# Delta-rule rounds: the small TensorE groups laid in 16 slots, TensorE held to the program order, two PSUM tiles for the group products

## The chip, the cores and the metric

The kernel runs on one core of one Trainium2 chip. The metric is the device time of that core in microseconds (us), the median of the runs. TensorE does the matmuls, VectorE and ScalarE the elementwise work, GpSimd a little setting to zero, and SyncE (SP) issues the DMAs.

## The reference

Two transformer blocks follow each other over 512 positions of width 1024. The change lies in the first block's gated delta rule (8 heads, 8 chunks of 64 positions):

```python
h = rms_norm(x, norm1_w) * (1 + scale1) + shift1
proj = h @ w_in
qkv = silu(causal_dwconv(concatenate([dn_q, dn_k, dn_v]), dn_conv_w))
...
a_mat = where(strict, einsum('bhncd,bhnjd->bhncj', k_beta, kc) * decay, 0.0)
sol = triangular_solve(eye + a_mat, rhs, left_side=True, lower=True, unit_diagonal=True)
u, w = sol[..., :dv], sol[..., dv:]
...
def step(state, inp):                      # over the 8 chunks
    qe_i, att_i, u_i, w_i, kd_i, dec_i = inp
    v_new = u_i - w_i @ state
    o_i = qe_i @ state + att_i @ v_new
    state = state * dec_i + kd_i.T @ v_new
    return state, o_i
...
o_a = rms_norm(o_a, dn_norm_w) * silu(dn_z)
y_a = o_a @ w_out_dn
```

Beside it stand the modulation vector of the block (`silu(c) @ w_ada + b_ada`), an attention, the feed-forward part, and the second block; these are as they were.

## The kernel before

**Dense work.** A projection (`proj`) makes a 128x512 tile in PSUM from 8 steps over the width, each of three matmuls, since weights and activations are split into a high and a low part (`mm3`, lines 307 to 310: `hi` with `hi`, `hi` with `lo`, `lo` with `hi`). I call each of these 24 a dense matmul. `wload` loads a weight tile (512 KB) on SP's queue into one of two `raw` buffers, ScalarE makes `hi` and VectorE `lo` (L295).

**Delta-rule stage.** It runs in six rounds, t = 0 to 5. Heads go in pairs p = 0 to 3. Round t holds the projections of pair t (six tiles in rounds 0 to 3, four gate tiles in 4 and 5, two more `z` tiles from round 2 on), the preparation of pair t-1 (`pre_steps`, rounds 1 to 4), and the recurrence over the chunks of pair t-2 (`chain_steps`, rounds 2 to 5). Parts of the modulation vector are interleaved (`ada_steps`, L338: `adraw` tiles on VectorE).

**Preparation of a pair.** `estep` and `sums` make decays and norms; `kkstep(b)` (b = 0, 1 for the two halves of four chunks) makes the products `kk` of keys and queries on half the array (L608), and VectorE the matrix `C` from them. The triangular solve starts from 16x16 blocks: `kkstep` writes these blocks of `C` to DRAM in 8 small DMAs per half, `load_bk` loads them as `BK`, turned so that one partition holds one block; `subst` inverts them in 15 steps of two VectorE instructions (L659 and L661, in place in `UK`); `wback` copies the transpose `XK` and writes `UK` and `XK` to DRAM, and loads both back into block-diagonal tiles by 32 small DMAs on SP's queue (`U` and `Xb` alternately, 16 for b = 0, then 16 for b = 1). `lvl_steps(b)` then builds the 64x64 inverse from the blocks: `s0` multiplies `Cl16` (a copy of parts of `C`) with `Xb`, `s1`, `s2`, `s3` and `s2` again follow, and `s5` and `s6` give `ut` and `wt`; each is a group `pp` of four 128-wide matmuls (L689). `tk` and `tv` transpose keys and values (`tpk`, `tpv`).

**Recurrence of a pair.** `state(c)` makes `pw` = `wt` times state and `pc` = query times state (L762, L769, half the array each); VectorE makes `vn`. `update(c)` makes `ss` (L779) and the second part of `pc` (L789); VectorE and ScalarE make the next state `S` and the output `o`. `post` normalises `o` and transposes it (`tpo`).

**What sets the order.** `merge` (line 196) gives every step of several lists a place between 0 and 1 and calls them in the order of these places; a projection tile is one step, 24 dense matmuls in a row. In its call (line 840) `pr`, the preparation up to `wback`, is spread over 0 to 0.68 of the round, `l0` = `lvl_steps(0)` over 0.7 to 1, and `late`, the `lvl_steps(1)` of the round before, over 0.04 to 0.27. Behind that, the scheduler of the framework orders the instructions on each engine anew, as it finds them ready. PSUM has one bank each for `ppre` (all of `kk`, `tpk`, `tpv`, `pp`), `pst`, the two tags of `pch` (`pw` and `pc`), and two each for `psS` and the dense tiles.

## Time and profile before

| what | value |
| --- | --- |
| median of 3 runs | 2168.42 us (2167.34 to 2168.75) |
| the profiled execution | 2166.97 us, span 2165.2 us |
| TensorE (PE) busy | 2135.2 us, 99% of the span |
| weight loads (PEld) | 1722.0 us, 80% |
| VectorE (DVE) | 1202.5 us, 56% |
| ScalarE (ACT) | 898.0 us, 41% |
| mean granted clock of TensorE | 0.995 |

Matmuls are pipelined, so that a record overlaps the next; what a matmul costs is read from start to start. Weight loads run beside the matmuls. Of the time from start to end TensorE is idle for 30 us, and most of that lies at the two ends. The delta-rule stage takes 380.5 us of the span.

### The profile page before, as it was taken

The numbers are of one execution on the slowest core, as the hardware profiler recorded it, in microseconds if no ns is written. First come the engines' busy times: TensorE is split into PE (matmuls) and PEld (weight loads), VectorE is DVE, ScalarE is ACT, GpSimd is POOL, SyncE is SP. The second block draws the span as 40 slices with busy tenths as digits, with TensorE's granted clock in tenths as the row PEclk, the third lists the DMA queues.
The fourth block names the chain that finished last, engine by engine and source line by source line (L and its number), as shares of the span: only waits on it lengthen the run. The fifth ranks groups of instructions, "written<-read, shape, count | busy, mean of one in ns | idle before, by whom it ended". The sixth has DMA issues, their size and how long they took to land.

```text
span 2165.2 us, 27498 instructions
## 1 busy us (share of the span) xinstructions
PE 2135.2 (99%) x10636; PEld 1722.0 (80%) x10636; DVE 1202.5 (56%) x2243; ACT 898.0 (41%) x1479; POOL 17.8 (1%) x49
## 2 busy tenths in 40 slices
PE   7999999999999999999999999999999999999997
PEld 3787877778888878888888887887778888888886
DVE  4777667465554554444335898545544454334446
ACT  5645443465553353333224323634443343224333
POOL 1000000000000000000000000000000000000000
PEclk9999999999999999999999999999999999999999
DMA  8533334222224343333333222232222433333332
GB/s 312 167 109 115 90 91 131 61 67 69 73 71 129 105 136 94 96 95 95 95 100 117 80 83 83 74 98 83 84 78 82 148 97 98 96 98 97 92 96 77
DMA packets 89579, 219.86 MB, mean 102 GB/s; under 512 B 23384, under 2 KB 28648, under 8 KB 88808
## 3 DMA queue, kind: packets, MB, share of 16 engines
q1 hardware_dynamic: 89448, 218.10, 33.0%
q8 instruction: 84, 1.38, 0.3%
q14 instruction: 47, 0.39, 0.1%
HBM read 211.50 MB, written 7.08 MB: 101 GB/s over the span
## 4 chain that ended last, share of the span: by engine, by line
PE 90%; DVE 5%; ACT 2%; issue 1%; DMA 1%; SPq 0%; DVEq 0%; ACTq 0%
PE mm L308 25%; PE mm L310 25%; PE mm L309 24%; PE pp L689 2%; DVE yc L1265 1%; DVE lo L295 1%; PE bpo L1593 1%; PE po L1041 1%; PE tps L1202 1%; PE tps L1203 1%; PE tps L1204 1%; PE ssp L571 1%; PE pw L762 1%; PE pc L789 1%; PE ss L779 1%
## 5 line engine op out<-in xcount | busy, mean ns | idle before, releaser
L294 ACT ACTIVATE hi<-raw 128x1024 fp32r<-128x1024 f32 (+3 forms) x354 | 351.5, 994 | 779.0 <-PE mm L309 690.4
L295 DVE TENSOR_TENSOR lo<-raw,hi 128x1024 fp32r<-128x1024 f32 (+3 forms) x354 | 403.8, 1141 | 439.0 <-ACT hi L294 427.9
L308 PE MATMUL mm<-H,hi 128*128 128x512 f32 x856 | 341.8, 400 | 4.7 <-ACT hi L294 1.7
L310 PE MATMUL mm<-H,lo 128*128 128x512 f32 (+1 forms) x856 | 340.5, 398 | 0.5 <-DVE lo L295 0.5
L309 PE MATMUL mm<-H,hi 128*128 128x512 f32 (+1 forms) x856 | 340.0, 397 | 0.0
L308 PEld LDWEIGHTS mm<-H,hi 128*128 128x128 f32 x856 | 161.4, 189 | 41.2 <-issue 3.0
L310 PEld LDWEIGHTS mm<-H,lo 128*128 128x128 f32 (+1 forms) x856 | 161.4, 189 | 36.1 <-issue 3.4
L309 PEld LDWEIGHTS mm<-H,hi 128*128 128x128 f32 (+1 forms) x856 | 161.5, 189 | 33.9 <-issue 2.7
L308 PE MATMUL mm<-XN,hi 128*128 128x512 f32 (+1 forms) x456 | 180.0, 395 | 0.0
L309 PE MATMUL mm<-XN,hi 128*128 128x512 f32 (+1 forms) x456 | 179.6, 394 | 0.0
L310 PE MATMUL mm<-XN,lo 128*128 128x512 f32 (+1 forms) x456 | 179.3, 393 | 0.0
L310 PEld LDWEIGHTS mm<-XN,lo 128*128 128x128 f32 (+1 forms) x456 | 85.1, 187 | 19.3 <-issue 1.7
L308 PEld LDWEIGHTS mm<-XN,hi 128*128 128x128 f32 (+1 forms) x456 | 85.1, 187 | 18.8 <-ACT hi L294 0.9
L309 PE MATMUL mm<-HN,hi 128*128 128x512 f32 x256 | 100.0, 391 | 0.0
L308 PE MATMUL mm<-HN,hi 128*128 128x512 f32 x256 | 99.6, 389 | 0.0
L310 PE MATMUL mm<-HN,lo 128*128 128x512 f32 x256 | 99.6, 389 | 0.0
L308 PE MATMUL mm<-F,hi 128*128 128x512 f32 x256 | 99.6, 389 | 0.0
L309 PE MATMUL mm<-F,hi 128*128 128x512 f32 x256 | 99.6, 389 | 0.0
L310 PE MATMUL mm<-F,lo 128*128 128x512 f32 x256 | 99.6, 389 | 0.0
L309 PEld LDWEIGHTS mm<-XN,hi 128*128 128x128 f32 (+1 forms) x456 | 84.9, 186 | 17.8 <-issue 1.3
L1265 DVE SCALAR_TENSOR_TENSOR yc<-cp,cdh,yc 128x512 f32<-128x512 f32 x120 | 89.9, 750 | 2.9
L308 PE MATMUL mm<-FF,hi 128*128 128x512 f32 x176 | 68.5, 389 | 0.0
(662 smaller groups left out, 3817.1 us busy)
## 6 DMA issues: line engine op xcount, KB each, us to landing
raw<-in_w_ff SPq DMA_DIRECT2D x64, 512.0 KB, 3.6
raw<-in_ffn_up SPq DMA_DIRECT2D x44, 512.0 KB, 3.6
raw<-in_w_dn SPq DMA_DIRECT2D x32, 512.0 KB, 3.8
adraw<-in_w_adaT SPq DMA_DIRECT2D x64, 256.0 KB, 3.2
raw<-in_w_ga SPq DMA_DIRECT2D x32, 512.0 KB, 3.7
raw<-in_w_br SPq DMA_DIRECT2D x32, 256.0 KB, 2.7
raw<-in_ffn_down SPq DMA_DIRECT2D x16, 448.0 KB, 3.4
X<-in_xT SPq DMA_DIRECT2D x4, 1024.0 KB, 7.2
```

The source lines that it names most:

```text
L294: nc.scalar.activation(out=hi, in_=src, func=AF.Copy)
L295: nc.vector.tensor_tensor(out=lo, in0=src, in1=hi.bitcast(F32), op=ALU.subtract)
L308: nc.tensor.matmul(ps, wh, xh, start=start, stop=False)
L309: nc.tensor.matmul(ps, wh, xl, start=False, stop=False)
L310: nc.tensor.matmul(ps, wl, xh, start=False, stop=stop)
L571: nc.tensor.matmul(ssp[64 * h:64 * h + 64, kind * 8 + c:kind * 8 + c + 1], sq[:, c], C("ones", 0, 1), start=True, stop=True)
L689: nc.tensor.matmul(pp[:, c4], lh[:, c4], rh[:, c4], start=True, stop=True)
L762: nc.tensor.matmul(pw[64 * h:64 * h + 64], st["wt"][b][:, c4, 64 * h:64 * h + 64], S[:, h], start=True, stop=True)
L779: nc.tensor.matmul(ss, st["kd"][b][64 * h:64 * h + 64, c4], vn[64 * h:64 * h + 64], start=True, stop=True)
L789: nc.tensor.matmul(pc[:, 0], ATT[(2 * p + b) % 4][:, c4], vn, start=True, stop=True)
L1041: nc.tensor.matmul(po[:, qs], VT[:, kb, hh], pT[:, kb * P:kb * P + P], start=(kb == 0), stop=(kb == qb))
L1265: i = nc.vector.scalar_tensor_tensor(out=ycs[m], in0=cps[m][:, s:s + T], scalar=cdh[:, m * 31 + s:m * 31 + s + 1], in1=ycs[m], op0=ALU.mul ...
```

## The change

Seven things are edited, all in the delta-rule stage.

1. `k_steps` cuts each projection tile into 8 steps of three dense matmuls.
2. `in_slots` takes the place of `merge` in rounds 1 to 5: a round has 16 slots. At the start of a slot come the small steps that a list names for it, in the order turns, chain, late levels, preparation, first levels, modulation; then a sixteenth of the dense steps (9 dense matmuls per slot in rounds 1, 4 and 5, 12 in rounds 2 and 3).
3. The places: `kkstep` in slots 2 and 3, `load_bk` 3, `subst` 4 to 7, `wback` 8, `lvl_steps(0)` from slot 10 to 14, `lvl_steps(1)` in slots 0 to 4 of the next round, and one step of the recurrence per slot.
4. `pin(True)` wraps TensorE's matmul and transpose, from round 1 to 5, so that the scheduler keeps them in the order of the program. The other engines are still ordered by the scheduler.
5. `ppre` has two buffers.
6. `pw` becomes a part of the `pc` tile, in one bank, and the `pc` product is issued ahead of it.
7. `post` is split: the transposes `tpo` become `turn`, which runs in slot 0 of the next round and takes its PSUM tile from `ppre`.

```diff
@@ -449,7 +449,7 @@
     dB = dctx.enter_context(pool("dB"))
...
     pst = dpx.enter_context(pool("pst", 1, PS))
-    ppre = dpx.enter_context(pool("ppre", 1, PS))
+    ppre = dpx.enter_context(pool("ppre", 2, PS))
     pch = dpx.enter_context(pool("pch", 1, PS))
@@ -521,8 +521,20 @@
     ST = [dict() for _ in range(4)]
...
-    def conv_silu(widx, dst):
-        ps = proj(PRE.pop(widx, A["w_dn"][widx]), H)
+    def k_steps(src, done):
+        st = {}
+        def one(k):
+            if k == 0:
+                st["w"] = src if isinstance(src, tuple) else wload(src, KD, P)
+                st["ps"] = PSM[0].tile([P, T], F32, tag="mm", name="mm")
+            mm3(st["ps"], st["w"][0][:, k], st["w"][1][:, k], H[0][:, k], H[1][:, k], k == 0, k == KD - 1)
+            if k == KD - 1:
+                done(st["ps"])
+        return [lambda k=k: one(k) for k in range(KD)]
+    def conv_silu(widx, dst, ps):
         acc = dA.tile([P, T], F32, tag="cacc", name="cacc", bufs=2)
@@ -533,30 +545,34 @@
     def proj_steps(p):
...
-        def one(kind, h):
+        def one(kind, h, ps):
             if "KQ" not in st:
...
             if kind == 0:
-                conv_silu(8 + 2 * p + h, st["KQ"][:, :, h])
+                conv_silu(8 + 2 * p + h, st["KQ"][:, :, h], ps)
             elif kind == 1:
-                conv_silu(2 * p + h, st["KQ"][:, :, 2 + h])
+                conv_silu(2 * p + h, st["KQ"][:, :, 2 + h], ps)
             else:
-                conv_silu(16 + 2 * p + h, st["vf"][:, :, h])
-        return [lambda kind=kind, h=h: one(kind, h) for kind in range(3) for h in range(2)]
+                conv_silu(16 + 2 * p + h, st["vf"][:, :, h], ps)
+        def tile_steps(kind, h):
+            w = (8, 0, 16)[kind] + 2 * p + h
+            done = lambda ps: one(kind, h, ps)
+            return k_steps(PRE.pop(w, A["w_dn"][w]), done)
+        return [tile_steps(kind, h) for kind in range(3) for h in range(2)]
...
-        def one(h):
+        def one(h, zps):
             zs = dB.tile([P, T], F32, tag=f"zs{h}", name=f"zs{h}")
-            zps = proj(A["w_dn"][24 + 2 * p + h], H)
             acts(func=AF.Silu, out=zs, in_=zps)
...
-        return [lambda h=h: one(h) for h in range(2)]
+        return [k_steps(A["w_dn"][24 + 2 * p + h], lambda ps, h=h: one(h, ps)) for h in range(2)]
@@ -740,11 +756,44 @@
         def gap():
...
-        early = ([estep, sums] + [lambda b=b: kkstep(b) for b in range(2)] + [load_bk]
-                 + [lambda f=f, b=b: f(b) for b in range(2) for f in (tk, tv)]
-                 + [lambda ks=ks: subst(ks) for ks in (range(15, 11, -1), range(11, 8, -1), range(8, 4, -1), range(4, 0, -1))]
-                 + [wback])
-        return early, lvl_steps(0), lvl_steps(1)
+        sub = [lambda ks=ks: subst(ks) for ks in (range(15, 11, -1), range(11, 8, -1), range(8, 4, -1), range(4, 0, -1))]
+        early = [(0, estep), (1, sums), (2, lambda: kkstep(0)), (3, lambda: kkstep(1)), (3, load_bk),
+                 (5, lambda: tk(0)), (5, lambda: tv(0)), (6, lambda: tk(1)), (6, lambda: tv(1)),
+                 (4, sub[0]), (5, sub[1]), (6, sub[2]), (7, sub[3]), (8, wback)]
+        def lvl(b, i0):
+            return [(i0 + d, f) for d, f in zip((0, 1, 1, 2, 3, 4, 4), lvl_steps(b))]
+        return early, lvl(0, 10), lvl(1, 0)
+    def in_slots(pj, *lists):
+        steps = [f for l in pj for f in l]
+        n = len(steps)
+        slots = [[] for _ in range(16)]
+        for l in lists:
+            for i, f in l:
+                slots[i].append(f)
+        at = 0
+        for i, s in enumerate(slots):
+            for f in s:
+                f()
+            end = (i + 1) * n // 16
+            for f in steps[at:end]:
+                f()
+            at = end
+    pinned = []
+    def pin(on):
+        if on:
+            for n in ("matmul", "transpose"):
+                f = getattr(nc.tensor, n)
+                pinned.append((n, f))
+                setattr(nc.tensor, n, lambda *a, f=f, **k: tc.keep_in_program_order(f(*a, **k)))
+        else:
+            for n, f in pinned:
+                setattr(nc.tensor, n, f)
+            pinned.clear()
@@ -757,16 +806,16 @@
                 st["vn"] = st["ut"][0][:, 0]
...
             S = st["S"]
-            pw = pch.tile([P, P], F32, tag="c1", name="pw")
+            pc = pch.tile([P, 3, P], F32, tag="c2", name="pc")
+            for h in range(2):
+                nc.tensor.matmul(pc[64 * h:64 * h + 64, 1], st["KQ"][:, c, 2 + h], S[:, h], start=True, stop=True)
+            pw = pc[:, 2]
             for h in range(2):
...
             st["vn"] = vn
-            pc = pch.tile([P, 2, P], F32, tag="c2", name="pc")
-            for h in range(2):
-                nc.tensor.matmul(pc[64 * h:64 * h + 64, 1], st["KQ"][:, c, 2 + h], S[:, h], start=True, stop=True)
             st["pc"] = pc
@@ -785,7 +834,7 @@
                         nc.vector.scalar_tensor_tensor(out=Sn[:, h], in0=S[:, h], scalar=egl[:, c, p:p + 1],
...
                 st["S"] = Sn
-            pc = st["pc"] if c else pch.tile([P, 2, P], F32, tag="c2", name="pc")
+            pc = st["pc"] if c else pch.tile([P, 3, P], F32, tag="c2", name="pc")
             nc.tensor.matmul(pc[:, 0], ATT[(2 * p + b) % 4][:, c4], vn, start=True, stop=True)
@@ -798,8 +847,11 @@
             o, os = st["o"], st["ss"]
...
             nc.vector.tensor_tensor(out=o, in0=o, in1=r.unsqueeze(2).to_broadcast([P, 8, P]), op=ALU.mult)
+        def turn():
+            o = st["o"]
             for b in range(2):
-                tp = pch.tile([P, 4, P], F32, tag="c2", name="tpo")
+                tp = ppre.tile([P, 4, P], F32, tag="pre", name="tpo")
                 for c4 in range(4):
@@ -809,25 +861,28 @@
                         scalar=V("dn_nw"), in1=st[f"zs{h}"][:, sl].rearrange("p (c t) -> p c t", t=64),
...
-        return [lambda f=f, c=c: f(c) for c in range(8) for f in (state, update)] + [post]
+        def begin():
+            state(0)
+            update(0)
+        return [begin] + [lambda f=f, c=c: f(c) for c in range(1, 8) for f in (state, update)] + [post, turn]
...
     def gate_steps(wg, ms, tiles, alloc):
-        def one(m):
+        def one(m, gp):
             if m % 4 == 0:
                 tiles.append(alloc())
-            gp = proj(A[wg][m], H)
             acts(func=AF.Tanh, out=tiles[m // 4][:, m % 4], in_=gp, scale=0.5)
-        return [lambda m=m: one(m) for m in ms]
+        return [k_steps(A[wg][m], lambda ps, m=m: one(m, ps)) for m in ms]
...
     NADA = (0, 2, 2, 2, 4, 6)
-    late = []
+    late, turns = [], []
     for t in range(6):
@@ -839,8 +894,17 @@
             pj[2:2] = z_steps(t - 2)
...
         ad, adas = adas[:na], adas[na:]
-        merge((0, 0.9, ch), (0, 0.68, pr), (0.7, 1, l0), (0.04, 0.27, late), pj, (0, 0.5, ad), (0, 0.6, g0))
+        if t == 0:
+            merge([lambda l=l: [f() for f in l] for l in pj], (0, 0.6, g0))
+        else:
+            if t == 1:
+                pin(True)
+            in_slots(pj, turns, [(min(i, 14), f) for i, f in enumerate(ch[:-1])], late, pr, l0,
+                     [(1 + i, f) for i, f in enumerate(ad)])
+            turns = [(0, ch[-1])] if ch else []
         late = l1
+    pin(False)
+    turns[0][1]()
     dpx.close()
...
```

The orders below are those in which the instructions stand on an engine. TensorE at `kkstep(1)` of round 2 (`kk` of 8 products), before:

```order
L689 MATMUL pp_1317<-Xb_975,Cl32_279 128x128 x4
L762 MATMUL pw_1488<-S_1436,wt_1119 64x128 x2
L769 MATMUL pc_1493<-S_1436,KQ_285 64x128 x2
L308 MATMUL mm_1837<-H_73,hi_1832 128x512
L309 MATMUL mm_1837<-H_73,hi_1832 128x512
L608 MATMUL kk_1323<-KQ_647 64x128 x8
L779 MATMUL ss_1523<-vn_1491,kd_785 128x128
L779 MATMUL ss_1526<-vn_1491,kd_785 128x128
L789 MATMUL pc_1493<-vn_1491,att0_270 128x128
L310 MATMUL mm_1837<-H_73,lo_1833 128x512
```

and after, where all of TensorE's instructions of rounds 1 to 5 carry the line of the wrapper, 792:

```order
L792 MATMUL mm_1354<-H_73,lo_1350 128x512
L792 MATMUL mm_1354<-H_73,hi_1349 128x512 x2
L792 MATMUL mm_1354<-H_73,lo_1350 128x512
L792 MATMUL pc_1367<-S_1295,KQ_310 64x128 x2
L792 MATMUL pc_1367<-S_1295,wt_1095 64x128 x2
L792 MATMUL pp_1374<-U_937,Pb2_1307 128x128 x4
L792 MATMUL kk_1380<-KQ_725 64x128 x8
L792 MATMUL mm_1354<-H_73,hi_1349 128x512 x2
L792 MATMUL mm_1354<-H_73,lo_1350 128x512
```

The parts of `state` and `update` that stood one by one between dense matmuls now stand together at the slot's start, with `pp` of the late levels and `kk`.

TensorE at `s0` of the first level in round 2 (`pp` from `Xb` and `Cl16`), before:

```order
L309 MATMUL mm_2487<-H_73,hi_2482 128x512
L689 MATMUL pp_1804<-Xb_1701,Cl16_278 128x128 x4
L310 MATMUL mm_2487<-H_73,lo_2483 128x512
L308 MATMUL mm_2487<-H_73,hi_2482 128x512
L309 MATMUL mm_2487<-H_73,hi_2482 128x512
L310 MATMUL mm_2487<-H_73,lo_2483 128x512
L689 MATMUL pp_1810<-Pb_1803,U_1700 128x128 x4
```

and after:

```order
L792 MATMUL mm_1685<-H_73,hi_1680 128x512 x2
L792 MATMUL mm_1685<-H_73,lo_1681 128x512
L792 MATMUL ss_1724<-vn_1703,kd_852 128x128
L792 MATMUL ss_1727<-vn_1703,kd_852 128x128
L792 MATMUL pc_1698<-vn_1703,att1_271 128x128
L792 MATMUL pp_1742<-Xb_1640,Cl16_278 128x128 x4
L792 MATMUL mm_1754<-H_73,hi_1749 128x512 x2
L792 MATMUL mm_1754<-H_73,lo_1750 128x512
L792 MATMUL mm_1754<-H_73,hi_1749 128x512 x2
```

The group stands behind `update` of chunk 4 (`ss` and `pc` from `vn_1703`) in slot 10; 84 dense matmuls stand between it and `kkstep(1)`, where 141 stood before.

VectorE at the end of the substitution in round 2 (`TK` and `UK`; then `XK`), before:

```order
L661 TENSOR_TENSOR UK_1399<-UK_1399,TK_1678 64x2x14
L284 SCALAR_TENSOR_TENSOR rst_1882<-rsy_1881 128x8
L280 TENSOR_SCALAR rsy_2071<-rsa_2070 128x16
L659 TENSOR_TENSOR TK_1681<-BK_1398,UK_1399 64x15
L285 TENSOR_TENSOR rst_1882<-rst_1882,rsa_1880 128x8
L281 TENSOR_SCALAR rsy_2071<-rsy_2071 128x16
L661 TENSOR_TENSOR UK_1399<-UK_1399,TK_1681 64x15
L286 SCALAR_TENSOR_TENSOR rsy_1881<-rst_1882,rsy_1881 128x8
L590 TENSOR_TENSOR GT_2813<-DC_256,G_259 128x512
L666 COPY XK_1696<-UK_1399 64x256
L284 SCALAR_TENSOR_TENSOR rst_1882<-rsy_1881 128x8
```

and after:

```order
L817 TENSOR_TENSOR vn_1703<-ut_1439,pc_1698 128x128
L677 TENSOR_TENSOR UK_1401<-UK_1401,TK_1603 64x2x14
L338 ISA adraw_3682,am_3632<-adraw_3682,cb_282 128x512
L338 ISA am_3632 128x1
L675 TENSOR_TENSOR TK_1606<-BK_1400,UK_1401 64x15
L342 TENSOR_TENSOR mod_60<-am_3632 128x4
L677 TENSOR_TENSOR UK_1401<-UK_1401,TK_1606 64x15
L343 TENSOR_TENSOR mod_60<-mod_60,VS_59 128x4
L682 COPY XK_1635<-UK_1401 64x256
L1200 SCALAR_TENSOR_TENSOR s2_62<-mod_60,VS_59 128x8
L834 SCALAR_TENSOR_TENSOR S_1723<-S_1623,eglA_263,ss_1724 128x128
L834 SCALAR_TENSOR_TENSOR S_1723<-S_1623,eglB_264,ss_1727 128x128
```

What stands between the last substitution steps has changed from the norm's small steps to `adraw` tiles and to `vn` of the recurrence.

## Rows read from the trace of the kernel before

**Rows 1.** Windows: us, PE, PEld, DVE, ACT, POOL busy (count), PEclk, DMA share, GB/s

```profile
68.40:448.90 380.50, 379.28 (x2335) 296.98 (x2334) 262.38 (x731) 179.38 (x369) 5.79 (x11) 1.00 0.34 103
183.20:237.10 53.90, 53.90 (x314) 40.87 (x314) 39.62 (x128) 24.48 (x48) 0.53 (x1) 0.97 0.26 76
342.20:387.00 44.80, 44.38 (x237) 33.48 (x238) 29.70 (x104) 14.81 (x35) 0.00 (x0) 1.00 0.35 101
```

**Rows 2.** TensorE's timeline: start, duration (us), engine, line, operation, out<-in, shapes, count

```profile
354.41 0.40 PE L309 MATMUL mm<-H,hi 128*128 128x512 f32 x1
354.74 0.44 PE L769 MATMUL pc<-S,KQ 128*64 128x128 f32 x4
355.11 0.50 PE L310 MATMUL mm<-H,lo 128*128 128x512 f32 x1
355.44 0.39 PE L308 MATMUL mm<-H,hi 128*128 128x512 f32 x1
355.67 0.60 PE L628 MATMUL tpk<-CS,KQ 128*128 128x128 f32 x4
356.20 0.49 PE L779 MATMUL ss<-vn,kd 64*128 64x128 f32 x4
356.62 0.49 PE L789 MATMUL pc<-vn,att 128*128 128x128 f32 x2
356.87 0.48 PE L309 MATMUL mm<-H,hi 128*128 128x512 f32 x1
```

**Rows 3.** Timelines of TensorE, SP's queue and VectorE along the chain of pair 2

```profile
262.39 1.09 PE L608 MATMUL kk<-KQ 128*64 128x128 f32 x16
...
270.23 0.47 SPq L650 DMA_DIRECT2D BK<-scr  x1
...
275.09 0.17 DVE L659 TENSOR_TENSOR TK<-BK,UK 64x15 f32<-64x15 f32 x1 [1.08 <-DMA BK<-scr]
...
299.06 0.16 DVE L661 TENSOR_TENSOR UK<-UK,TK 64x15 f32<-64x15 f32 x1
...
299.25 0.46 SPq L668 DMA_DIRECT2D scr<-UK  x1
...
309.98 0.42 SPq L681 DMA_DIRECT2D Xb<-scr  x1
```

**Rows 4.** DMA issues: out<-in, queue, operation, count, KB each, us to landing

```profile
Xb<-scr SPq DMA_DIRECT2D x64, 4.0 KB, 1.7
```

**Rows 5.** TensorE's timeline where `pp` (Xb, Cl16) runs, pair 2

```profile
314.69 0.39 PE L308 MATMUL mm<-H,hi 128*128 128x512 f32 x1
314.92 1.05 PE L689 MATMUL pp<-Xb,Cl 128*128 128x128 f32 x8
...
316.04 0.39 PE L310 MATMUL mm<-H,lo 128*128 128x512 f32 x1
```

**Rows 6.** TensorE's timeline at one `pw` half by itself

```profile
357.97 0.43 PE L762 MATMUL pw<-S,wt 128*64 128x128 f32 x2
358.33 0.51 PE L310 MATMUL mm<-H,lo 128*128 128x512 f32 x1
```

**Rows 7.** VectorE's groups, 77 to 449 us: busy, mean ns, idle before

```profile
L295 DVE TENSOR_TENSOR lo<-raw,hi 128x1024 fp32r<-128x1024 f32 (+1 forms) x40 | 48.3, 1207 | 21.5 <-ACT hi L294 21.1 <-issue 0.2
L529 DVE SCALAR_TENSOR_TENSOR cacc<-mm,VS,cacc 128x509 f32<-128x509 f32 (+2 forms) x61 | 45.1, 741 | 4.2 <-ACT cacc L527 4.1
L338 DVE CUSTOM_DVE_ANT_0 adraw<-adraw,cb 128x512 f32<-128x512 f32 x56 | 38.1, 683 | 6.3 <-DMA adraw<-in_w_adaT 6.3
L659 DVE TENSOR_TENSOR TK<-BK,UK 64x15 f32<-64x15 f32 (+7 forms) x60 | 11.5, 192 | 2.0 <-DMA BK<-scr 1.8
L785 DVE SCALAR_TENSOR_TENSOR S<-S,eglA,ss 128x128 f32<-128x128 f32 x24 | 8.2, 343 | 6.0 <-PE ss L779 5.9
```

**Rows 8.** Windows of the two stretches at the lower clock (columns as in rows 1)

```profile
219.60:223.00 3.40, 3.40 (x10) 2.63 (x9) 1.29 (x8) 0.00 (x0) 0.00 (x0) 0.50 0.17 39
35.30:42.10 6.80, 6.80 (x20) 5.13 (x20) 4.52 (x11) 1.28 (x2) 0.00 (x0) 0.50 0.69 235
```

## The prediction, made blind

> **What bounds the kernel now.** I read the windows of the delta stage first. From 68.4 to 448.9 us TensorE is busy for 379.28 of 380.50 us, VectorE for 262.38 and ScalarE for 179.38 [rows 1]. So TensorE sets the time, and every microsecond that it gains or waits is one of the kernel's. What it spends there has three parts: 987 dense matmuls at 0.227 to 0.23 us from start to start, the small groups between them, and the price of changing between the two. Next I read TensorE's timeline for that price [rows 2], then the one chain of the stage that leaves the chip's engines, the write-back of the 16x16 inverses through DRAM [rows 3, 4], because the change fixes how much TensorE work stands beside it.
>
> That chain is what the reader should look at. It starts when `kkstep(1)` ends (262.39 + 1.09 = 263.48), goes through VectorE (`C`), eight small writes on SP's queue, the load `BK` (issued 270.23), thirty substitution steps on VectorE (first 275.09, last done 299.22), the write of `UK` (299.25), and then loads `U` and `Xb` alternately on SP's queue, the eighth `Xb` issued at 309.98 [rows 3] and landing 1.7 us after [rows 4]. Only then may `s0` of the first level start (`pp<-Xb,Cl`, 314.92 [rows 5]). In the four rounds of before, 50 us or so lie between; the two that I list are 53.90 and 44.80 [rows 1]. TensorE loses nothing by it: the scheduler has put 189, 141, 138 and 131 dense matmuls between `kkstep(1)` and that `pp` (counted in its order), far past where the code has them.
>
> **Part 1: fewer changes of shape (gain).** A full 128-wide group costs nearly what it computes: `pp` of 4 in the dense stream takes 316.04 - 314.69 = 1.35 us less two dense steps of 0.23, 0.89, against 8 records of about 0.11 [rows 5]. A half-array group (`pw`, `pc` from `S`, `kk`, `ssp`, `ss`) is dearer: dense to `pc` 0.33 instead of 0.23 (+0.10), out again 0.37 for 0.17 of work (+0.20), and the next dense step 0.33 (+0.10, where a full group leaves about +0.09); a change inside a group, `tpk` to `ss`, costs about +0.10 [rows 2]. Counted in both orders between dense matmul 113 and 1049: entries from dense 53 before and 56 after, exits to dense 60 and 23, changes inside a group 77 and 57; breaks of the dense stream 133 and 72. That is 37 x 0.21 - 3 x 0.10 + 20 x 0.10 = 9.5 us less. Halves that now stand side by side add to it: 18 `pw` products stand alone in before, where one half takes 0.36 (357.97 to 358.33 [rows 6]), as long as two take together, so nine pairs save about 0.2 each, 1.8; and the `ssp` columns come in four groups of 32 instead of eleven of 8 or 16, about 2.9 less. Sum **-14 us**; all of it lies on TensorE, which sets the end. No step is added to TensorE; `pc` and `pw` merely share a tile.
>
> **Part 2: the pinned order (loss).** `s0` now stands in slot 10 and `kkstep(1)` in slot 3, and nothing behind `s0` in TensorE's order may pass it. What stands between them is 63, 84, 84 and 63 dense matmuls in rounds 1 to 4. At 0.229 that is 14.4 or 19.2 us. The small groups there: in round 1 the two pairs of transposes, 1.8; in rounds 2 to 4 also two `pp` groups (1.8), three `state` (0.8 each) and four `update` groups (0.85 each), 9.3 together. So TensorE reaches `s0` **16.2, 28.5, 28.5 and 23.7 us** after `kkstep(1)`.
>
> The chain takes, from rows of before: `kkstep(1)` end to first substitution step 275.09 - 263.48 = 11.6; last step to the eighth `Xb` landed 309.98 - 299.22 + 1.7 = 12.5 [rows 3, 4]. Between them VectorE must do what its order now puts from the first step to the last. In round 2: 30 steps x 0.192 = 5.8, seven `adraw` x 0.683 = 4.8, two weight splits x 1.207 = 2.4, two 512-wide products at about 0.74 = 1.5, and eight small ones (`S`, `o`, `vn`) at about 0.34 = 2.7, together 17.2. Round 1: 5.8 + 4.8 + three convolution steps x 0.741 = 12.8. Round 3: 5.8 + 0.7 + 1.2 + 1.5 + six small = 11.2. Round 4: 5.8 + 2.4 + 1.5 + 2.7 = 12.4 [rows 7]. The chain is then 36.9, 41.3, 35.3 and 36.5 us, and TensorE waits **21, 13, 7 and 13 us, 53 together**.
>
> Bounds. Below: the steps run alone (5.8), which makes the chain 29.9. Round 1 still waits 14 and round 3 about 1; in rounds 2 and 4 `XK` stands on VectorE behind `vn` of chunk 5, which TensorE releases only in slot 9, one slot before `s0` (some 3 us), so these wait about 9 whatever VectorE does. Sum 34. Above: the steps are stretched as in before, 299.22 - 275.09 = 24.1 us; the waits are then 32, 20, 20 and 24, 96. I take 53, because the order lists the work between, and it is less than in before (50 rows instead of 66 in round 1, 43 instead of 72 in round 3). While TensorE waits, the dense matmuls behind `s0`, the `conv` work that reads them on ScalarE and VectorE, and the weight splits that wait for their buffers all wait with it, so nothing is made up later: behind the wait TensorE sets the pace again.
>
> **Part 3: what goes and what comes besides.** Priced by these steps, the stage of before is 373.6 us, and it took 380.5 [rows 1]: 6.9 us of waits and slow clock, of which I let half go, **-3** (0 to -7). `tpo` moves to slot 0 of the next round behind 18 or 24 dense matmuls, 4.1 or 5.5 us, and `post` needs about 5 on VectorE, so at most 1 us; with one bank for `pw` and `pc`, `state(c+1)` also waits for `o` of chunk c, a copy and a sum of about 0.35 each one slot earlier, covered by 2.1 to 2.8 us of dense matmuls. I put **+1** for both (0 to 6). The second `ppre` bank lets two groups stand back to back and costs nothing. SP's queue keeps its 32 loads per round; the two weight loads that stand before them are enough for the next tiles.
>
> The clock: before the change there is a spell at half speed, 219.60 to 222.99, granted 0.50 (1.2 of 2.4 GHz), in which eight dense steps took 0.43 each (3.40 / 8) instead of 0.23: 1.6 us; TensorE had been busy ahead of it with narrow `ssp` columns. The longer spell, 35.30 to 42.10, lies in the load phase, where TensorE had idled [rows 8]. The stage of before has no wait of this length, so the term is bounded by 0 and by four long spells, 4 x 16 steps x 0.2 = 13. I take one short spell behind each of the three longest waits, **+5**. The Trainium skill (TensorE: Matmul & The Clock Gate, section HAM oscillation — how this bites in real kernels) speaks against the change here: it says that a wait for a DMA between bursts of matmuls sends the clock down, and the next burst begins at half rate. By that rule the term is sure; were only the spell of row 219.60 to go by, it could be 0, and the sum 5 less.
>
> **Sum.** The profiled execution took 2166.97 us (span 2165.2), 1.45 under the median of the runs, 2168.42. 2166.97 - 14 + 53 - 3 + 1 + 5 = 2210; rounded down a little, since the bounds of the largest term lie nearer below (34) than the order makes likely above, **2208 us**, 1.8% slower.
>
> **Rivals.** *The chain is covered* (faster): `UK` is done by slot 7 and the loads land while TensorE still has dense matmuls. For it: VectorE has 30% idle in this stage. Against it: even with the steps run alone the rows give 34 us of waits, and 17 would have to be left for the time to be the same as before. If the waits vanish, 2166.97 - 14 - 3 = 2150. It decides where the chain is shorter than 16 to 28 us.
> *VectorE becomes the bound instead*, in rounds 1 and 2: its rows of round 1 sum to 56 us and of round 2 to 83, priced as above, against 46 and 77 us of TensorE; 15 us more, and if the chain then hides behind this, 2166.97 - 14 - 3 + 15 = 2165. Against it: much of that sum is `adraw` work that can slide.
> *The clock stays down longer*: every one of the four waits is followed by a spell like 35.30 to 42.10. That is 13 in place of 5: 2216 us. For it: TensorE idles for 7 us and more each time.
> *The edit does nothing* is excluded: the new order shows `s0` at slot 10, with a DMA among the things that it waits for.
>
> **How the numbers follow.** The forecast 0.68, the longer spells 0.15, the covered chain 0.12, VectorE's bound 0.05. The forecast's own range goes from 2166.97 - 14 - 7 + 34 = 2180 towards 2166.97 - 14 + 96 + 13 = 2262, of which I leave out the end where all VectorE work stretches as in before. Range 2174 to 2240, which holds all but the covered chain, part of the third case and some of the upper end. A measurement of this kernel tells about 0.2% (4 us) from no change: faster 0.12, same 0.05, slower 0.83.
>
> **What would show it.** Right: in the profile after, TensorE idles once in each of four rounds ahead of a `pp<-Xb,Cl` group, 7 to 21 us, first round longest, and what ends it is the DMA of `Xb`; the granted clock is 0.5 just behind; the stage's other TensorE steps are shorter by some 14 us, with no single-half product left; the busy share of TensorE in the stage falls to about 88%. Wrong: idle time that ends with VectorE's `vn`, `S` or a weight split in most slots (the second rival), or none to speak of (the first). The prediction falls if VectorE finishes `UK` in slot 7, or if small loads issued in a row take much less than 0.47 us each.

## The result: 2.6% slower, and where the time went

The changed kernel takes 2223.14 us (median of 4 runs, 2221.87 to 2226.04) against 2168.28 us. The ratio to before is 1.0258, 95% interval 1.0245 to 1.0271. The forecast was 2208 us, slower by 1.8%, in a range of 2174 to 2240. The sign, the mechanism and the range held; of the 55 us, 40 were forecast. Beside the runs that follow, the kernel before took 2166.98 to 2167.19 us, and their ratios are to that.

The profiled execution took 2221.87 us (span 2220.1). TensorE's busy time is 2139.7 us, 4.5 more than before, and 96% of the span. The views below answer to those ahead of the prediction, on the same stretch: from and to the same dense matmuls as [rows 1].

Windows of the kernel after: the delta-rule stage, then the nine stretches in it at the lower clock (us, PE, PEld, DVE, ACT, POOL busy with counts, PEclk, DMA share, GB/s).

```profile
67.88:503.13 435.25, 383.41 (x2336) 306.77 (x2334) 273.26 (x733) 177.91 (x369) 5.79 (x11) 0.92 0.31 90
89.50:96.33 6.83, 5.46 (x27) 4.64 (x26) 4.50 (x19) 3.35 (x5) 0.00 (x0) 0.50 0.51 156
120.22:144.12 23.90, 3.45 (x12) 3.19 (x13) 10.04 (x42) 1.33 (x5) 0.00 (x0) 0.50 0.31 86
171.42:178.25 6.83, 6.54 (x40) 5.85 (x41) 4.78 (x19) 0.76 (x2) 0.00 (x0) 0.50 0.46 144
219.21:229.45 10.24, 4.25 (x14) 3.80 (x15) 2.34 (x7) 2.18 (x7) 0.00 (x0) 0.50 0.10 10
256.75:260.17 3.42, 3.17 (x11) 2.56 (x12) 2.52 (x7) 1.73 (x5) 0.00 (x0) 0.50 0.00 0
270.41:273.82 3.41, 3.41 (x10) 2.63 (x9) 2.41 (x14) 0.00 (x0) 0.00 (x0) 0.50 0.50 154
314.78:318.19 3.41, 2.80 (x11) 2.63 (x12) 0.39 (x1) 1.34 (x3) 0.00 (x0) 0.50 0.10 12
355.74:359.15 3.41, 3.41 (x12) 2.14 (x11) 1.96 (x13) 0.00 (x0) 0.00 (x0) 0.50 0.00 0
393.29:403.53 10.24, 4.10 (x14) 3.65 (x15) 0.00 (x0) 1.49 (x5) 0.00 (x0) 0.50 0.11 11
```

Read the first row against [rows 1]: the stage is 435.25 - 380.50 = 54.75 us longer, which is the whole loss. TensorE is idle in it for 435.25 - 383.41 = 51.84 us, where it was 1.22. The clock is the second item: before had one stretch at 0.50 in this stage [rows 8], after has nine, in which TensorE was busy for 36.6 us (the sum of the nine PE columns). I call such a stretch a spell.

TensorE's waits in the stage, kernel after (line and tile, what it waited for: us in total, times, longest).

```profile
PE pp L792 <- DMA Xb<-scr: 44.0, 4, 22.9
PE tpo L792 <- DVE o L849: 2.9, 2, 2.4
PE ssp L792 <- ACT dsq L585: 2.2, 2, 1.4
```

The first row is the forecast one: four waits, one in each round, ahead of `pp<-Xb,Cl`, ended by the DMA of `Xb`. They are 22.9, 8.6, 3.9 and 8.5 us long; 21, 13, 7 and 13 were forecast. The first stands in the chain below; the other three in TensorE's timeline:

```profile
225.20 2.05 PE L792 MATMUL pp<-Xb,Cl 128*128 128x128 f32 x8 [8.64 <-DMA Xb<-scr]
315.39 2.04 PE L792 MATMUL pp<-Xb,Cl 128*128 128x128 f32 x8 [3.93 <-DMA Xb<-scr]
399.43 2.05 PE L792 MATMUL pp<-Xb,Cl 128*128 128x128 f32 x8 [8.51 <-DMA Xb<-scr]
```

The chain of pair 0 (round 1) in the timelines of TensorE, SP's queue and VectorE, as in [rows 3]; in square brackets the idle time before and what ended it.

```profile
99.97 1.09 PE L792 MATMUL kk<-KQ 128*64 128x128 f32 x16
...
109.67 0.54 SPq L666 DMA_DIRECT2D BK<-scr  x1
...
115.72 0.16 DVE L675 TENSOR_TENSOR TK<-BK,UK 64x15 f32<-64x15 f32 x1
...
128.59 0.16 DVE L677 TENSOR_TENSOR UK<-UK,TK 64x15 f32<-64x15 f32 x1
...
129.11 0.47 SPq L684 DMA_DIRECT2D scr<-UK  x1
...
138.60 0.42 SPq L697 DMA_DIRECT2D Xb<-scr  x1
...
140.67 2.05 PE L792 MATMUL pp<-Xb,Cl 128*128 128x128 f32 x8 [22.91 <-DMA Xb<-scr]
```

From the end of `kk` (101.06) to `pp` lie 39.6 us: 14.7 to the first substitution step, 13.0 for the thirty steps, 11.9 for the write-back. TensorE was there after 16.7 us and stood still for 22.9.

### The profile page after: what moved, and what is told of

It is laid out like the page before. It is cut to its first block, busy times and chain, and to the rows that moved or that the text cites. A ratio compares the mean times of both kernels' runs of the same rounds, so it can differ in the third digit from the quotient of the medians.

```text
span 2220.1 us, 27515 instructions
## 1 busy us (share of the span) xinstructions
PE 2139.7 (96%) x10636; PEld 1731.9 (78%) x10636; DVE 1212.7 (55%) x2243; ACT 896.0 (40%) x1479; POOL 17.8 (1%) x49
## 4 chain that ended last, share of the span: by engine, by line
PE 86%; DVE 6%; ACT 3%; DMA 2%; issue 2%; SPq 1%; DVEq 0%; ACTq 0%
PE mm L308 21%; PE mm L309 21%; PE mm L310 21%; PE mm L792 7%; PE pp L792 2%; DVE lo L295 1%; DVE yc L1329 1%; PE pc L792 1%; PE bpo L1657 1%; DMA adraw<-in_w_adaT 1%; PE po L1105 1%; PE tps L1266 1%; PE tps L1267 1%; PE tps L1268 1%; ACT hi L294 1%
## 5 line engine op out<-in xcount | busy, mean ns | idle before, releaser
L308 PE MATMUL mm<-H,hi 128*128 128x512 f32 x584 | 229.9, 394 | 5.9 <-ACT hi L294 1.7
L310 PE MATMUL mm<-H,lo 128*128 128x512 f32 (+1 forms) x584 | 229.3, 393 | 0.5 <-DVE lo L295 0.5
L309 PE MATMUL mm<-H,hi 128*128 128x512 f32 (+1 forms) x584 | 229.1, 392 | 0.0
L792 PE MATMUL mm<-H,hi 128*128 128x512 f32 x544 | 184.4, 421 | 0.0
L308 PEld LDWEIGHTS mm<-H,hi 128*128 128x128 f32 x584 | 109.9, 188 | 31.6 <-ACT hi L294 2.7
L310 PEld LDWEIGHTS mm<-H,lo 128*128 128x128 f32 (+1 forms) x584 | 109.9, 188 | 24.0 <-DVE lo L295 1.0
L309 PEld LDWEIGHTS mm<-H,hi 128*128 128x128 f32 (+1 forms) x584 | 109.9, 188 | 23.6 <-DVE H L295 0.5
L792 PEld LDWEIGHTS mm<-H,hi 128*128 128x128 f32 x544 | 101.8, 197 | 23.7 <-issue 5.4
L792 PE MATMUL mm<-H,lo 128*128 128x512 f32 x272 | 109.7, 403 | 0.0
L308 PEld LDWEIGHTS mm<-XN,hi 128*128 128x128 f32 (+1 forms) x456 | 85.1, 187 | 18.9 <-ACT hi L294 0.9
```

The source lines that it names most:

```text
L308: nc.tensor.matmul(ps, wh, xh, start=start, stop=False)
L309: nc.tensor.matmul(ps, wh, xl, start=False, stop=False)
L310: nc.tensor.matmul(ps, wl, xh, start=False, stop=stop)
L792: setattr(nc.tensor, n, lambda *a, f=f, **k: tc.keep_in_program_order(f(*a, **k)))
```

## Experiments: the waits at s0

I had two theories. The first: the pin fixes `s0` ahead of its DMA, and this wait is the loss. The rival: the slots, VectorE's order or the bank that `pw` and `pc` share make the loss, and `s0` is only where it shows.

**The pin left out (x1_free).**

```diff
-            if t == 1:
-                pin(True)
```

> The changed kernel with the pin left out: same slots, same tiles, but the scheduler may move TensorE's instructions again. Its order then has 227, 135, 131 and 125 dense matmuls between kkstep(1) and the pp of s0, where the changed kernel has 63, 84, 84 and 63. Theory (the pin fixes s0 ahead of its DMA): the four waits on Xb (44.0 us) and the slow clock behind them (about 7 us) vanish, and some of the saved changes of shape stays: 2155 to 2175 us, and no idle time over 1 us ahead of a pp. Rival (the slots themselves, VectorE's order or the bank that pw and pc share make the loss): 2200 us or more, with idle time that moves elsewhere.

Measured: 2165.18 us (median of 10 runs), ratio to before 0.999 (0.9981 to 1.0). Its stage, by the windows view, and the three stretches at the lower clock in it:

```profile
68.44:448.81 380.37, 379.69 (x2335) 301.95 (x2334) 266.25 (x733) 178.83 (x369) 5.78 (x11) 0.97 0.34 103
91.07:97.90 6.83, 6.83 (x37) 5.20 (x37) 2.59 (x11) 0.00 (x0) 0.00 (x0) 0.50 0.26 89
213.95:220.78 6.83, 6.83 (x29) 5.26 (x28) 2.60 (x13) 1.48 (x2) 0.00 (x0) 0.50 0.20 59
295.87:302.70 6.83, 6.83 (x30) 5.54 (x29) 4.17 (x20) 0.63 (x1) 0.00 (x0) 0.50 0.10 10
```

With slots and tiles as in the change, but the scheduler's order, TensorE is idle for 0.68 us. So the rival falls: without the pin nothing of the loss is left. But nothing is gained either, although the small groups stand together. The rows say where that gain is: TensorE is busy throughout three slow stretches, 20.5 us, where before had 3.4. (The profiled execution took 2167.64 us at a mean clock of 0.991, the ten runs 2163.47 to 2168.77 at 0.991 to 0.993, so that the number of slow stretches can differ from one run to the next.)

**The data of `s0` not awaited (x3_no_load).**

```diff
-                nc.gpsimd.memset(U, 0.0)
-                nc.gpsimd.memset(Xb, 0.0)
+                nc.gpsimd.memset(U, 0.01)
+                nc.gpsimd.memset(Xb, 0.01)
+                DU = dA.tile([P, 4, 16], F32, tag="DU", name="DU")
+                DX = dA.tile([P, 4, 16], F32, tag="DX", name="DX")
...
-                        nc.sync.dma_start(out=U[r0:r0 + 16, :, r0:r0 + 16],
+                        nc.sync.dma_start(out=DU[r0:r0 + 16],
...
-                        nc.sync.dma_start(out=Xb[r0:r0 + 16, :, r0:r0 + 16],
+                        nc.sync.dma_start(out=DX[r0:r0 + 16],
```

> The changed kernel, pin and all, but U and Xb hold a constant, and the 32 small loads of each pair go to a tile that nobody reads (the inverse is left out of the result). Nothing on TensorE waits for the write-back any more. Theory (the write-back chain is what ends last at s0): 44.0 us of waits and about 7 us of slow clock go: 2172 us (2165 to 2180), TensorE idle some 8 us in the stage. Rival (another step, VectorE's S and vn or the weight splits, stands close behind and takes the wait over): 2195 us or more.

Measured: 2169.77 us, ratio to before 1.0011 (1.0002 to 1.002). TensorE keeps the pinned order, and its stage is

```profile
68.17:449.94 381.77, 375.23 (x2336) 299.57 (x2334) 270.02 (x730) 178.60 (x369) 5.80 (x11) 0.97 0.34 102
```

with 6.5 us idle. Nothing takes the wait over: VectorE, the weight splits and the recurrence keep up with the pinned order as it is. So the wait on the write-back, with the slow clock behind it, is what makes the kernel slower. Four spells are left in this stage, all of them at `ssp`, in which TensorE worked 20.3 us.

**`s0` three slots later (x10_s0_late).** Here the pin stays and the place moves; the steps of the level stand between the dense steps of a slot.

```diff
-            return [(i0 + d, f) for d, f in zip((0, 1, 1, 2, 3, 4, 4), lvl_steps(b))]
+            ds = (0, 0.7, 0.7, 1.3, 2, 2.6, 2.6) if b == 0 else (0, 1, 1, 2, 3, 4, 4)
+            return [(i0 + d, f) for d, f in zip(ds, lvl_steps(b))]
...
-        return early, lvl(0, 10), lvl(1, 0)
+        return early, lvl(0, 13), lvl(1, 0)
...
-                slots[i].append(f)
+                slots[int(i)].append((i % 1, f))
...
+            s = sorted(s, key=lambda x: x[0])
+            for j in range(at, end):
+                while s and s[0][0] * (end - at) <= j - at:
+                    s.pop(0)[1]()
+                steps[j]()
```

> The changed kernel, pinned, with the first levels later: s0 at slot 13 in place of 10, the other steps of the level at 13.7 to 15.6 (between the dense steps of a slot). 90, 120, 120 and 90 dense matmuls then stand between kkstep(1) and s0, and TensorE comes there about 6.2 us later in rounds 1 and 4 and 10.6 us in rounds 2 and 3, which covers all of the waits of 8.6, 3.9 and 8.5 but for some 2 of the last, and 6.2 of the 22.9. Theory (the loss is the place of s0): 25 us of waits less, 5 of slow clock behind the three that go, 11 more breaks at 0.3: 2223 - 25 - 5 + 3 = 2196 us (2190 to 2202). Rival (the chain from kkstep to Xb is paced by TensorE's own groups, so that it gets longer when s0 does): the waits stay, 2215 us or more.

Measured: 2190.13 us, at the low end of what was expected, ratio to before 1.0106 (1.0092 to 1.0119). Its stage, and TensorE's wait on the DMA:

```profile
67.97:471.51 403.54, 379.42 (x2335) 302.45 (x2334) 271.46 (x733) 179.10 (x369) 5.79 (x11) 0.95 0.33 97
```

```profile
PE pp L796 <- DMA Xb<-scr: 18.0, 1, 18.0
```

One wait of four is left, that of round 1, which has 90 dense matmuls to cover a chain of 41.6 us. Sum of TensorE's idle time 24.1 us. The place of `s0` in a fixed order decides. How the chain grows with it shows only in round 1, where TensorE still waits for it: 41.6 us in place of 39.6.

## Experiments: the clock

TensorE's idle time grew by 51.84 - 1.22 = 50.6 us. That leaves 54.75 - 50.6 = 4 us, where the fewer changes of shape alone should have left -14. Two causes of a lower clock were open: the waits, and something at the norm's products `ssp`, where four of the nine stretches begin.

**Dense work in the waits (x4_fill).**

```diff
+                if b == 0:
+                    fill = ppre.tile([P, T], F32, tag="pre", name="fill")
+                    for _ in range((96, 35, 15, 35)[p]):
+                        nc.tensor.matmul(fill, H[0][:, 0, 0:P], H[0][:, 0], start=True, stop=True)
                 pp = bdmm(Cl16, st["X"][b])
```

> The changed kernel with 96, 35, 15 and 35 additional dense matmuls into an unused tile ahead of s0 of the first level of the four pairs, so that TensorE works through most of each wait (22.0, 8.0, 3.4 and 8.0 us of 22.9, 8.6, 3.9 and 8.5). Theory (the waits lower the clock): the four spells at 0.5 that begin in or at these waits go, in which TensorE worked 14.6 us: 14.6 x 0.47 = 7 us less, 2216 us. Rival (the clock there falls for another reason, or costs nothing): 2223 us, or more if the additional work runs slower than the wait was long.

Measured: 2221.14 us, 2 us less than the kernel after; 7 were expected. Windows of its stage and of the four places at `s0`:

```profile
67.90:502.41 434.51, 420.88 (x2517) 336.65 (x2515) 273.82 (x735) 178.64 (x369) 5.79 (x11) 0.96 0.31 90
...
120.22:144.12 23.90, 22.99 (x106) 18.89 (x105) 10.30 (x44) 2.44 (x7) 0.00 (x0) 1.00 0.33 90
212.00:229.45 17.45, 16.77 (x94) 13.56 (x93) 7.45 (x18) 4.42 (x11) 0.00 (x0) 1.00 0.18 31
311.69:318.52 6.83, 5.58 (x17) 4.84 (x18) 0.00 (x0) 1.50 (x5) 0.00 (x0) 0.50 0.10 9
391.00:403.50 12.50, 11.09 (x54) 8.98 (x53) 0.82 (x3) 2.43 (x9) 0.00 (x0) 1.00 0.09 9
```

At three of the four places the clock stays at 1.00: an idle TensorE was the cause there. At the third, a wait of 4.2 us was left, and the spell with it. The three spells held 3.45 + 4.25 + 4.10 = 11.8 us of work, in which a dense step takes 0.43 instead of 0.23; 11.8 x (1 - 0.23 / 0.43) = 11.8 x 0.47 = 5.5 us should be saved. The third spell and those elsewhere became longer, so that TensorE's work at 0.50 fell by 8.1 us, from 36.6 to 28.5; times 0.47 that is 3.8. Without the 181 additional matmuls at 0.23, 41.6 us, TensorE is busy for 420.88 - 41.6 = 379.3 us, 4.1 less than in the kernel after. So the slow clock costs what its rows say. But idle time of 434.51 - 420.88 = 13.6 and the 41.6 are 55.2 together, where 51.84 stood: 3.4 more. That is round 3, whose chain took 36.4 us from `kk` to `pp` in place of 32.7: with the edit, other work stands between the substitution steps in VectorE's order (12.4 us for the thirty steps in place of 10.2), and the loads of `U` and `Xb` begin later behind it. In the other three rounds the chain is within 1 us of what it was.

**The norm's products apart (x5_ssp_apart).**

```diff
-        def sums():
+        def sums(s):
...
-        early = [(0, estep), (1, sums), (2, lambda: kkstep(0)), (3, lambda: kkstep(1)), (3, load_bk),
+        early = [(0, estep)] + [(f, lambda s=s: sums(s)) for s, f in enumerate((0.3, 0.6, 1, 1.3))] + [(2, lambda: kkstep(0)), (3, lambda: kkstep(1)), (3, load_bk),
...
```

`in_slots` is edited as in x10_s0_late, so that a step can stand between the dense steps of its slot.

> The changed kernel with the norm's 32 one-column products (ssp) in four groups of 8 products, each behind at least three dense matmuls, instead of all in a row. Theory (the row of narrow products lowers the clock: four of the nine slow spells of the stage begin in or right behind one): these four spells go, TensorE worked some 18 us in them: 18 x 0.47 = 8.6 us less, 2.2 us of waits for the squares less, and 12 more breaks of the dense stream at about 0.3 each, 3.6 more: 2216 us. Rival (the clock does not answer to these products): 2223 to 2227 us with the spells still there.

Measured: 2236.37 us, ratio to before 1.0316 (1.03 to 1.0331). I missed here, in the direction too. Its stage and the five spells at these products:

```profile
67.81:516.54 448.73, 393.37 (x2335) 311.75 (x2334) 272.62 (x730) 179.26 (x369) 5.79 (x11) 0.91 0.30 87
89.11:99.35 10.24, 10.24 (x54) 7.70 (x55) 3.99 (x17) 4.43 (x5) 0.00 (x0) 0.50 0.28 82
171.03:177.86 6.83, 6.83 (x39) 5.74 (x40) 1.88 (x7) 4.46 (x5) 0.00 (x0) 0.50 0.19 55
270.02:273.43 3.41, 3.41 (x16) 2.33 (x16) 0.29 (x1) 2.47 (x3) 0.00 (x0) 0.50 0.53 169
358.77:365.59 6.82, 6.82 (x40) 5.73 (x39) 0.86 (x2) 2.54 (x3) 0.00 (x0) 0.50 0.25 76
369.01:372.42 3.41, 3.41 (x13) 2.36 (x11) 1.57 (x9) 0.00 (x0) 0.00 (x0) 0.50 0.00 0
```

The spells are where they were, longer, and one more (two in round 4): that the products stand in one row isn't what lowers the clock. TensorE's busy time grows by 10 us and its idle time by 3.5.

**The same products, 32 columns wide (x6_wide).** This leaves their number, place and order as in the change.

```diff
-                    nc.tensor.matmul(ssp[64 * h:64 * h + 64, kind * 8 + c:kind * 8 + c + 1], sq[:, c],
-                                     C("ones", 0, 1), start=True, stop=True)
-            a, r = rsqrt(dB, ssp[:, 0:16], 16, 1.0, EPS)
+                    nc.tensor.matmul(ssp[64 * h:64 * h + 64, 32 * (kind * 8 + c):32 * (kind * 8 + c) + 32], sq[:, c],
+                                     C("ones", 0, 32), start=True, stop=True)
+            a, r = rsqrt(dB, ssp.rearrange("p (n w) -> p n w", w=32)[:, :, 0], 16, 1.0, EPS)
```

> The changed kernel, same order on TensorE, but the norm's products (ssp) are 32 columns wide instead of one (the same number of products, in the same place; VectorE reads every 32nd column). Theory (products of one column lower the clock; it is not their place, nor that they stand in a row): the four spells at 0.5 that begin at ssp go; TensorE was busy for 18.8 us in them, 18.8 x 0.47 = 8.8 us less: 2214 us (2211 to 2218), with the spells at the waits still there. Rival (the clock falls there because so many small groups stand close together, whatever their width): 2223 us, spells unchanged.

Measured: 2212.54 us, 10.6 less than the kernel after. TensorE's timeline at the products of round 4, first of the kernel after, then of this one:

```profile
351.17 3.69 PE L792 MATMUL ssp<-CS,dsq 128*64 128x1 f32 x64
354.79 0.73 PE L792 MATMUL mm<-H,hi 128*128 128x512 f32 x2
...
356.74 1.05 PE L792 MATMUL mm<-H,hi 128*128 128x512 f32 x2
```

```profile
342.44 3.74 PE L792 MATMUL ssp<-CS,dsq 128*64 128x32 f32 x64
346.11 0.73 PE L792 MATMUL mm<-H,hi 128*128 128x512 f32 x2
...
347.61 0.61 PE L792 MATMUL mm<-H,hi 128*128 128x512 f32 x2
```

The 64 records (two of each product) take the same 3.6 to 3.7 us, one column or 32. But the pair of dense matmuls some steps behind takes 1.05 us after the narrow ones and 0.61 after the wide ones. The stage of this kernel, and the spells in it:

```profile
68.23:493.53 425.30, 376.46 (x2335) 300.12 (x2334) 274.40 (x733) 178.75 (x369) 5.80 (x11) 0.94 0.31 92
118.43:142.33 23.90, 5.25 (x16) 4.52 (x17) 9.02 (x38) 2.52 (x7) 0.00 (x0) 0.50 0.28 76
214.01:224.25 10.24, 5.53 (x17) 4.79 (x18) 1.25 (x5) 2.12 (x6) 0.00 (x0) 0.50 0.10 9
306.17:309.58 3.41, 3.03 (x11) 2.86 (x12) 0.36 (x1) 1.56 (x4) 0.00 (x0) 0.50 0.10 12
384.67:394.91 10.24, 5.89 (x19) 4.60 (x21) 0.59 (x1) 3.04 (x7) 0.00 (x0) 0.50 0.10 10
```

Four spells are left, all at the waits on `Xb`; the four at `ssp` are gone, and with them the one at 256.75. The width (and the stride with which VectorE reads the sums) is all that the edit changes, and four spells and 10.6 us went with it. In the stage 7.0 us of this are busy time (TensorE's work at 0.50 fell from 36.6 to 19.7 us), and 3.0 are idle time: the waits for ScalarE's squares (2.2) are gone, and those on `Xb` are 1.4 shorter. TensorE had not waited ahead of the third and fourth of these spells, so a wait isn't needed for the clock to fall. Why the spell at 256.75, behind a wait of 2.4 us for `tpo`, went as well is open; the wait is still there.

What remains open too is why the kernel before, with the same one-column products, has one such spell and not four. In three of its four rounds they stand in groups of 32, 16 and 16 records, as in the three rounds of x1_free that have a spell. The first two groups start 4.0, 4.4 and 3.3 us apart in before and 3.1, 2.6 and 2.6 in x1_free. No run varies this distance and nothing else.

## Experiments: what the change is worth without the pin

The norm can also be made with 16 products over the full array. x7_full and x8_full_wide do so on x1_free, with one and with 32 columns; x9_before_full does it, with one column, on the kernel before.

```diff
-                kind, h = divmod(s, 2)
-                sq = dA.tile([P, 8, 64], F32, tag="dsq", name="dsq", bufs=2)
-                nc.scalar.activation(out=sq, in_=st["KQ"][:, :, s], func=AF.Square)
-                for c in range(8):
...
+                kind, half = divmod(s, 2)
+                sq = dA.tile([P, 4, 2, 64], F32, tag="dsq", name="dsq", bufs=2)
+                nc.scalar.activation(out=sq, in_=st["KQ"][:, 4 * half:4 * half + 4, 2 * kind:2 * kind + 2], func=AF.Square)
+                for c4 in range(4):
+                    n = kind * 8 + 4 * half + c4
+                    nc.tensor.matmul(ssp[:, n:n + 1], sq[:, c4].rearrange("p h t -> p (h t)"),
+                                     C("ones", 0, 1), start=True, stop=True)
```

> The changed kernel without the pin (x1_free, 2165.2 us), with the norm's sums made by 16 products over the full array (both heads' squares side by side) in place of 32 on half of it, one column each. The products take half as long: 4 x 1.8 = 7.2 us less, and some 12 changes to half the array at about 0.2 go, 2.4: 2156 us, if the three slow spells of that kernel stay. Theory (one-column products lower the clock, the more of them the more): with half of the narrow time some or all spells go, 20.5 x 0.47 = 9.6 us at most: 2146 to 2156. Rival (the clock answers to changes of shape in general): no less than 2156 with the three spells kept.

> As x7_full, with 32 columns per product. Theory (narrow columns): no slow spell is left in the delta-rule stage: 2165.2 - 7.2 - 2.4 - 9.6 = 2146 us (2143 to 2150). Rival (crowding of small groups): the spells stay, 2156 us.

> The kernel before, with the full-array products of x7_full alone and nothing else of the change. 7.2 us and some 2 us of shape changes less, and its one spell (1.6 us): 2157 us (2155 to 2160). If the part of the change that x1_free keeps (steps of one slot together, pc and pw in one tile) is worth the 8 us that its trace shows at full clock, x8_full_wide is some 10 us faster than this; if that part is worth nothing, the two are equal.

Measured: 2158.35, 2155.61 and 2162.33 us, ratios to before 0.9958 (0.9943 to 0.9972), 0.9945 (0.9931 to 0.996) and 0.9984 (0.9974 to 0.9994). The spells in the stages of the profiled executions: one, none, none, against three in x1_free. That x8_full_wide has none is as the theory has it, and it takes less time than both kernels. All three sums were too low, by 2 to 12 us for x7, 10 for x8 and 5 for x9, and one row shows most of why. TensorE's timeline of x8_full_wide at the first eight products of a round:

```profile
284.05 1.87 PE L588 MATMUL ssp<-CS,dsq 128*128 128x32 f32 x16
285.75 0.48 PE L308 MATMUL mm<-H,hi 128*128 128x512 f32 x1
```

16 records take 1.70 us, 0.106 each, where the half-array ones took 3.62 / 64 = 0.057. Half as many products at twice the price: the 7.2 us that I counted for them weren't there. It is the same with one column (16 records in 1.70 us in x7_full). So x7_full spends nearly as long on one-column products as x1_free and yet has one spell and not three. Whether their number does this or the width of the array that they use, no run separates.

**The tiles alone (x12_one_tile), beside x8_full_wide again (x13_best_again).** The kernel before with x8's norm and, of the change, two PSUM edits: no slots, no steps of three matmuls, no pin.

```diff
-    ppre = dpx.enter_context(pool("ppre", 1, PS))
+    ppre = dpx.enter_context(pool("ppre", 2, PS))
...
-            pw = pch.tile([P, P], F32, tag="c1", name="pw")
+            pc = pch.tile([P, 3, P], F32, tag="c2", name="pc")
+            for h in range(2):
+                nc.tensor.matmul(pc[64 * h:64 * h + 64, 1], st["KQ"][:, c, 2 + h], S[:, h], start=True, stop=True)
+            pw = pc[:, 2]
...
```

> The kernel before with the full-array norm products, 32 columns wide, and of the change only the PSUM part: two ppre tiles, and pw inside the pc tile with the pc product first. No slots, no steps of three dense matmuls, no pin. In its order the dense stream of the stage breaks 128 times; 169 in x9_before_full, 120 in x8_full_wide. Theory (the tiles, not the slots, let the small groups stand together): nearly all of the 6.7 us between those two: 2157 us (2155 to 2159). Rival (the slots do it): 2162 us.

> x8_full_wide once more, beside x12_one_tile on the same chip: 2155.6 us (2154 to 2157), with no slow spell in the delta-rule stage.

Measured: 2153.79 us (ratio to before 0.9935, 0.9922 to 0.9947) and 2155.32 us (0.9943, 0.9929 to 0.9956). Their stages by the windows view, x9_before_full first, then x12_one_tile and x13_best_again (each with the same 2208 records of TensorE):

```profile
69.26:444.11 374.85, 374.24 (x2208) 295.96 (x2208) 262.33 (x732) 179.10 (x370) 5.78 (x11) 1.00 0.33 103
```

```profile
67.69:434.21 366.52, 365.75 (x2208) 294.79 (x2207) 265.05 (x731) 178.19 (x369) 5.77 (x11) 1.00 0.35 106
```

```profile
69.25:437.25 368.00, 367.48 (x2208) 295.43 (x2207) 265.71 (x731) 178.40 (x369) 5.79 (x11) 1.00 0.35 105
```

All three run at full clock and wait for less than a microsecond. x12_one_tile took 3 us less than its sum. The two PSUM edits together bring 8.3 us, and the slots beside them nothing more: the stage of x13_best_again is 1.5 us longer. The scheduler puts the groups together by itself, with 128 breaks of the dense stream where the order of x9_before_full has 169. Whether the second `ppre` bank does this or the tile that `pw` and `pc` share, no run separates; nor was a kernel run with the slots and without the tiles. x12_one_tile has the lowest time of all the kernels here: 13 us under the kernel before, 69 under the changed one.

## Why the prediction was right, and where its size was off

| term | forecast | measured in the stage |
| --- | --- | --- |
| fewer changes of shape | -14 | about -11.5 (what is left over) |
| waits at `s0` | +53 | +44.0 |
| waits and clock of before that go | -3 | -1.2 idle, -1.6 clock |
| other waits | +1 | +7.8 (51.84 - 44.0) |
| clock | +5 | about +17 (36.6 x 0.47) |
| sum | +42 | +54.75 |

The number came nearer than its terms: the waits at `s0` were 9 us too high, and the clock (12), the other waits (7) and the gain (2.5) together some 21 too low. That the errors partly cancel is luck. The sum as written is 2209 and not 2210, and its four lower bounds of the waits add up to 33 and not 34; neither moves the forecast.

**The mechanism was right.** Of the signs that were named, the four waits ahead of `pp<-Xb,Cl`, the DMA that ends them, the clock of 0.50 behind them and the busy share (383.41 / 435.25 = 88%) are there. The third wait, 3.9 us, is shorter than the 7 named.

**The place of TensorE was right to 1 us.** It came to `s0` 16.7, 28.7, 28.7 and 24.6 us after `kkstep(1)`; 16.2, 28.5, 28.5 and 23.7 were counted from the order. That is what an order under a pin is good for: it holds.

**The chain was right within 4 us.** 39.6, 37.4, 32.7 and 33.1 us against 36.9, 41.3, 35.3 and 36.5. The substitution took 13.0, 15.0, 10.2 and 12.7 (12.8, 17.2, 11.2 and 12.4 forecast from the instructions between its steps in VectorE's order), so the middle value was the right choice between alone (5.8) and stretched as in before (24.1). The write-back took 11.9 to 11.0 for 12.5, up to `pp`; the front took 14.7, 11.2, 10.8 and 9.4 for 11.6. Each wait is what the chain is longer than TensorE's way to `s0`, so that an error of 4 us in the chain is one of 4 us in a wait of 8.

**The clock is the term that failed.** I took one short spell behind each of three long waits, 5 us, and bounded it by four spells, 13. The waits did bring spells, whose cost by the rows is 14.6 us of work x 0.47 = 7. But four others begin at `ssp`, 18.8 us of work, 9 us, and I had the sign of it in hand: the one spell of the stage before [rows 8] stood behind narrow `ssp` products, I said so, and drew nothing from it for an order that puts all 32 together in each round. x6_wide gave back 10.6 us by their width, 7.0 of it in busy time. The factor of 0.47 holds in the other runs: TensorE's work at 0.50 in the stage falls from the kernel after by 16.3 us in x3_no_load, 8.1 in x4_fill, 16.9 in x6_wide and 8.3 in x10_s0_late, times 0.47 that is 7.7, 3.8, 7.9 and 3.9, and its busy time falls by 8.2, 4.1, 7.0 and 4.0. The third rival had the right item, the clock, and put it at the wrong place, behind the waits alone; its 2216 us lies nearer to what was measured than 2208.

**The small waits** were sized at 1 and are 7.8: `tpo` 2.9, where at most 1 was forecast, `ssp` for ScalarE's squares 2.2, which I hadn't listed (in round 1 the last of the four squares stands behind a table load of 1.28 us and the activation of `E` on ScalarE), 1.7 for a `cacc` step of VectorE in round 0, ahead of the pin, where before had 0.5, and the rest below 1 each.

**The gain was there.** By what is left over in the table it is 11.5 us, near the 14 that were counted; the single prices of part 1 were not measured one by one. Busy time at full clock gives the same by another way: 379.28 busy before less 1.6 of slow clock is 377.7; x3_no_load has 375.23 less 20.3 x 0.47, 365.7, and x6_wide 376.46 less 19.7 x 0.47, 367.2, which is 12.0 and 10.5 less. In x1_free the gain was hidden by the clock: 379.69 less 20.5 x 0.47 = 9.6 is 370.1. In x12_one_tile, against x9_before_full, it is 8.3.

The first rival (a covered chain) and the second (VectorE's bound) fell with the waits row: the idle time ended with the DMA, and x3_no_load, with VectorE's work as it was, ran in 2169.77.

## What to carry to other kernels

Before an engine is held to a written order, count for each of its waiting instructions the work that stands between cause and wait, and set it against the chain's own length read from the old trace: here this gave each wait to within 5 us, and their sum to within 9. An order that packs the small work tightly needs its clock counted too, product by product: look at what stands ahead of each slow spell in the old trace, and ask whether the change makes more of it. And try the buffers before the order: with the two PSUM edits alone the scheduler gave what the slots were written for.
